# The modulation products of a diffusion layer take silu(c) from PSUM, and the projections share six banks

## The chip, the cores and the metric

The kernel runs on one core of a Trainium2 chip. The metric is device time in microseconds (us); the times below are of whole executions, and the profile is of one further execution. The engines are called as in the profile: PE (TensorE) with its weight loads PEld, DVE (VectorE), ACT (ScalarE), POOL (GpSimd) and SP (SyncE), whose queue issues most of the DMAs. PSUM has eight banks; a bank holds 512 float32 values for each of 128 partitions.

## The reference

One layer works on 1024 latent tokens and 256 context tokens, with 1024 channels, in float32. What matters here is the first part:

```python
mod = jax.nn.silu(c) @ w_mod[l] + b_mod[l]
shift1, scale1, gate1, shift2, scale2, gate2 = jnp.split(mod[:, None, :], N_MOD, axis=-1)
...
mod_c = jax.nn.silu(c_ctx) @ w_mod[l, :, :n_mod_c * D_MODEL] + b_mod[l, :n_mod_c * D_MODEL]
...
h_c = ctx * (1.0 + mods_c[1]) + mods_c[0]
kv_ctx = _context_kv(h_c, w_in[l], b_in[l], k_norm_g[l])
h = x * (1.0 + scale1) + shift1
y = _latent_token_mixer(h, kv_ctx, w_in[l], b_in[l], attn_sink[l], q_norm_g[l], k_norm_g[l],
                        w_branch_a[l], w_branch_b[l], w_out[l], rope)
```

So a vector of 1024 values, silu(c), is multiplied with a matrix of 1024 x 6144 (and silu(c_ctx) with its first 2048 columns). The results scale and shift the tokens. The mixer then projects the tokens to queries, keys, values and gate logits (`proj = h @ w_in + b_in`), runs two attentions (a windowed one, A, and a global one, B), and merges them by sigmoid gates. An output projection, a layer norm, a convolutional feed-forward part and a second layer norm follow; the change does not touch these.

## The kernel before

**Precision.** Every large product is made of three matmuls on rounded parts (`mm3`, L379 to L381): high x high, high x low and low x high. `split` (L371, L376) makes the parts: a cast gives the high part, a subtraction the low one.

**The products with silu(c)** do not go through PE. `mod` (L478, L479) is one DVE instruction: it multiplies a tile of 128 x 1024 modulation weights, in SBUF, with silu(c) spread over all partitions (`sc`, or `scc` for the context's vector, both 128 x 1024 in SBUF), adds the bias and sums each partition's row into one column of `modc` or `modx`. There are 64 such columns. The first 16 (scale1 and shift1) are made in `modulate` (L501) at the very start, since the projections need them. The other 48 (`late`, first 16 with `scc`, then 32 with `sc`) are spread over the projections: `mods` (L941) is called after each step of PE work and issues as many products as are due, so that all are traced by the end of group ka. `mload` (L935) loads the next weight tile on SP when a product has been issued.

**The start.** PE spreads c over the partitions with a matmul against ones into two tiles `cb`, ACT makes silu of each half into `sc`, and warm-up matmuls run into `cb[1]` and into a tile `warm`.

**The projections**, in PE's order: first q of branch B ("q1acc", eight tiles of 128 tokens, weights stepped over eight channel blocks k); then gates ("g", each gate block in two halves of 512 tokens, 24 matmuls a half), and between them qa and qb (q of branch A, four tiles each), ka (keys and values of tokens 0 to 639, five tiles) and kb (tokens 640 to 1023 and the context, five tiles). `GORD` (L39) sets it: 3 gate blocks, qa, 4, qb, 4, ka, 1, kb, 3 (a fourth is kept for attention). So the halves are 6, 8, 8, 2 and 6. A group's tiles are all open from its first step to its last.

**Evictions.** A gate half is evicted by ACT's sigmoid (L967). q tiles are evicted by DVE at the end of their group (L607, L609). A key tile runs through `kv_post` (L670): s1 evicts it (DVE, L675) and makes sums of squares and the rotation of half of it; s2 finishes norm and rotation and splits the keys (L375, L376); s3 turns them by four PE transposes into a tile `ktr` (L706) that ACT copies away (L709, L711). `side_step` (L979) advances these pieces by one step after each PE step, and after ka the transposes of the first two units' queries (`qtr`, L741) go through the same queue. In the program the side steps stand so that ktr0 comes ahead of kb, ktr1 after kb's first step, ktr2 and qtr0 after its second, ktr3 and qtr1 after its third, ktr4 after its fourth.

**PSUM.** All these tiles come from `acc_tile` (L439): pool `ps1` has one tag with eight slots of one bank, and the framework gives a tile any slot that is free. When ps1 is released (L1064), attention's pool ps2 takes the banks.

**What sets the order.** The framework orders each engine's instructions at compile time, by the program's order and by when it reckons an instruction can start. Where a block of `manual_schedule` stands, the program's order is kept: for DVE and SP from the end of q1 to the end of ka (L1006, L1018), and for all engines in attention, which a planner in the kernel orders. PE's and ACT's orders in the projections, and DVE's after ka, are the framework's. Weights are loaded five steps ahead of their use (WLOAD) and split three steps ahead (WSPLIT).

## Time and profile before

| | |
|---|---|
| median of 3 runs | 1515.82 us (1514.42 to 1516.7) |
| span of the profiled execution | 1514.0 us |
| PE busy | 1501.8 us, 7584 matmuls |
| DVE busy | 1154.9 us |
| ACT busy | 799.4 us |
| POOL busy | 782.8 us |
| the 48 late products on DVE | 60.6 us to 243.4 us |

The profile is one execution. Busy time is the time in which an engine had an instruction of the program under way; a matmul's end is modelled, and matmuls overlap, so the distance between two starts tells more of PE's pace than the duration. A row of a group reads: line, engine, operation, tiles written and read (numbers left out), shapes, count, then busy us and mean ns of one, then the engine's idle time just before and what ended it. A row of a tile's view gives the shortest, median and longest duration in ns, and the first and last start in us. A timeline row gives start and duration in us. A row of a window gives its length and each engine's busy us with its number of instructions.

### The profile page before, as it was taken

Reading aid. Unit: us, or ns where it says so; the run is one execution under the profiler, and the core shown is the slowest. Engines: PE = TensorE matmul, PEld = TensorE weight load, DVE = VectorE, ACT = ScalarE, POOL = GpSimd, SP = SyncE. Lnnn points to the kernel's source line nnn. Section 1 sums busy time; section 2 is a strip of 40 time slices with the busy share of each in tenths; the row PEclk is TensorE's granted clock in tenths of the full one; section 3 lists DMA queues with packets and bytes.
Section 4 is the critical chain, followed back from the end, with each engine's and each line's share of the span. In section 5 each row is a group of like instructions: output and inputs, shape, how many; then the busy total and the mean of one; then the engine's idle time right before and its main releaser. Section 6 shows DMA issues by size and latency. Waiting matters only on the chain.

```text
span 1514.0 us, 21879 instructions
## 1 busy us (share of the span) xinstructions
PE 1501.8 (99%) x7584; PEld 1261.5 (83%) x7584; DVE 1154.9 (76%) x1735; ACT 799.4 (53%) x1406; POOL 782.8 (52%) x744
## 2 busy tenths in 40 slices
PE   9999999999999999999999999999999999999997
PEld 7888888889888888888888998888888888888886
DVE  7588847629887777787666888988888888657897
ACT  6422223449987777788233665444444444435533
POOL 0374303439996666576424446666676774021063
PEclk9999999999999999999999999999999999999999
DMA  9767773312447555623460322333344447996723
GB/s 377 269 211 257 223 238 108 99 42 68 125 135 180 147 119 139 148 60 117 141 166 22 113 89 98 112 111 112 112 111 112 112 111 199 367 271 205 252 83 112
DMA packets 112432, 229.84 MB, mean 152 GB/s; under 512 B 13537, under 2 KB 27617, under 8 KB 112226
## 3 DMA queue, kind: packets, MB, share of 16 engines
q1 hardware_dynamic: 97312, 199.85, 40.5%
q0 software_dynamic: 10400, 20.19, 8.6%
q10 hardware_dynamic: 4610, 8.42, 1.5%
q8 instruction: 59, 0.97, 0.3%
q14 instruction: 51, 0.42, 0.1%
HBM read 177.23 MB, written 65.87 MB: 161 GB/s over the span
## 4 chain that ended last, share of the span: by engine, by line
PE 94%; DVE 3%; issue 1%; DMA 1%; ACT 1%; POOL 0%; DVEq 0%; SPq 0%; ACTq 0%; POOLq 0%
PE av L864 7%; PE pt L855 7%; PE g L379 4%; PE g L380 4%; PE g L381 4%; PE s L762 3%; PE p L380 3%; PE s L763 3%; PE p L381 3%; PE p L379 3%; PE c L381 2%; PE d L381 2%; PE a L381 2%; PE d L379 2%; PE a L379 2%; PE c L380 2%
## 5 line engine op out<-in xcount | busy, mean ns | idle before, releaser
L1253 DVE TENSOR_TENSOR lo<-pt,hi 128x512 fp32r<-128x512 f32 x188 | 127.0, 687 | 47.7 <-ACT hi L1247 36.8
L376 DVE TENSOR_TENSOR ld<-rd,hd 128x1024 fp32r<-128x1024 f32 x77 | 97.6, 1285 | 49.6 <-ACT hd L371 47.5
L1247 ACT CAST hi<-pt 128x512 fp32r<-128x512 f32 x188 | 108.2, 583 | 41.1 <-PE av L864 23.6
L371 ACT CAST hd<-rd 128x1024 fp32r<-128x1024 f32 x77 | 79.5, 1050 | 86.3 <-PE p L381 57.6
L380 PE MATMUL p<-ld,hd 128*128 128x512 f32 x264 | 102.9, 390 | 0.6 <-DVE ld L376 0.6
L379 PE MATMUL p<-hd 128*128 128x512 f32 x264 | 103.3, 391 | 0.0
L381 PE MATMUL p<-hd,ld 128*128 128x512 f32 x264 | 102.8, 390 | 0.0
L864 PE MATMUL av<-hi,VT 128*128 128x512 f32 x236 | 101.1, 431 | 0.2 <-POOL hi L1242 0.2
L379 PE MATMUL g<-hh,whg 128*128 128x512 f32 x256 | 99.9, 390 | 0.0
L864 PE MATMUL av<-lo,VT 128*128 128x512 f32 x236 | 99.5, 428 | 0.2 <-POOL lo L1253 0.2
L380 PE MATMUL g<-hl,whg 128*128 128x512 f32 x256 | 99.7, 390 | 0.0
L381 PE MATMUL g<-hh,wlg 128*128 128x512 f32 x256 | 99.7, 389 | 0.0
L376 POOL TENSOR_TENSOR wlg<-wg,whg 128x512 fp32r<-128x512 f32 x32 | 45.4, 1423 | 100.8 <-ACT whg L371 88.4
L801 DVE TENSOR_SCALAR_CACHE_REDUCE p<-s,cvt,nmc 128x1024 f32<-128x1024 f32 x64 | 85.6, 1339 | 7.3 <-PE pt L855 4.3
L810 ACT ACTIVATE p<-p,nm 128x1024 f32<-128x1024 f32 x64 | 74.0, 1156 | 8.0 <-DVE p L801 7.9
L855 PEld LDWEIGHTS pt<-ident,p 128*128 128x128 f32 x512 | 63.5, 140 | 17.6 <-ACT rb L837 0.4
L855 PE MATMUL pt<-ident,p 128*128 128x128 f32 x512 | 76.6, 272 | 0.1
L762 PE MATMUL s<-KL,q 128*128 128x512 f32 (+2 forms) x186 | 73.8, 397 | 0.0
L371 ACT CAST wS<-s 128x512 fp32r<-128x512 f32 x76 | 45.2, 620 | 50.8 <-POOL s L1583 50.0
L763 PE MATMUL s<-KL,q 128*128 128x512 f32 (+2 forms) x186 | 69.6, 374 | 0.0
L371 ACT CAST wA<-ru 128x512 fp32r<-128x512 f32 x57 | 35.5, 623 | 62.3 <-PE d L381 34.1
L1253 POOL TENSOR_TENSOR lo<-ptr,hi 128x512 fp32r<-128x512 f32 x48 | 62.2, 1296 | 3.3
(437 smaller groups left out, 5007.0 us busy)
## 6 DMA issues: line engine op xcount, KB each, us to landing
wml<-in_wmodT_dram SPq DMA_DIRECT2D x48, 512.0 KB
ru<-in_w_up_dram SPq DMA_DIRECT2D x38, 512.0 KB
rd<-td SPq DMA_DIRECT2D x55, 256.0 KB
rd<-sd SPq DMA_DIRECT2D x44, 256.0 KB
rd<-in_w_dn_dram SPq DMA_DIRECT2D x33, 256.0 KB
wm<-in_wmodT_dram SPq DMA_DIRECT2D x16, 512.0 KB
wg<-in_w_g_dram SPq DMA_DIRECT2D x32, 256.0 KB
q<-q SPq DMA_DIRECT2D x64, 128.0 KB
```

Source lines behind the costliest of these rows:

```text
L371: cast[:] = [nc.scalar.copy(hi, src).ins]
L376: low[:] = [lo_eng.tensor_tensor(out=lo, in0=src, in1=hi.bitcast(F32), op=ALU.subtract).ins]
L379: nc.tensor.matmul(ps, a[0], b[0], start=start, stop=False, skip_group_check=resumed)
L380: nc.tensor.matmul(ps, a[0], b[1], start=False, stop=False, skip_group_check=resumed)
L381: return nc.tensor.matmul(ps, a[1], b[0], start=False, stop=stop, skip_group_check=resumed).ins
L762: nc.tensor.matmul(o, self.q1[:, hs], ks, start=True, stop=False)
L763: nc.tensor.matmul(o, self.q2[:, hs], ks, start=False, stop=stop)
L801: nc.vector.tensor_scalar(out=p if self.br else p[:, self.pad + 1:SINK + 1], in0=self.sv[h], scalar1=self.scale()[:, hs] if self.br else - ...
L855: nc.tensor.transpose(tr[:, h * P:(h + 1) * P], src, ident)
L864: nc.tensor.matmul(self.av, v, self.parts[n][low], start=first, stop=self.left == 0)
L1247: nc.scalar.copy(hi, units[u].parts[n])
L1253: e.tensor_tensor(out=lo, in0=src, in1=hi.bitcast(F32), op=ALU.subtract)
```

## The change

The PSUM pool gets named tags: six of one bank, used in turn by `acc_tile`, and one, "wide", of two banks. The wide tile serves first the two halves of `cb`, then the last two of q1's eight tiles, and then, in the late products, silu(c_ctx) and after it silu(c): ACT copies the row from SBUF into it, in two halves, when the first product with that row is issued (products 0 and 16 of the 48), and the products read it there. The 16 products at the start still read `sc` in SBUF.

```diff
-    ps1 = tc.alloc_tile_pool(name="ps1", bufs=8, space=PSUM, reuse_waits="tile")
+    ps1 = tc.alloc_tile_pool(name="ps1", bufs=1, space=PSUM, reuse_waits="tile")
+    abanks = list(range(6))
 
     def acc_tile(name, dt=F32):
-        return ps1.tile([P, 512], dt, tag="acc", name=name)
+        n = abanks.pop(0)
+        abanks.append(n)
+        return ps1.tile([P, 512], dt, tag=f"acc{n}", name=name)
+
+    def wide_tile(name):
+        return ps1.tile([P, T], F32, tag="wide", name=name)
...
-    cb = [acc_tile(f"cb{n}") for n in (0, 1)]
+    cbw = wide_tile("cb")
+    cb = [cbw[:, n * HALF:(n + 1) * HALF] for n in (0, 1)]
...
-    acc = [acc_tile(f"q1acc{t}") for t in range(NT)]
+    acc = [acc_tile(f"q1acc{t}") for t in range(6)]
+    accw = wide_tile("q1accw")
+    acc += [accw[:, n * HALF:(n + 1) * HALF] for n in (0, 1)]
...
+    crows = {}
+
+    def crow_psum(row, nm):
+        t = wide_tile(nm)
+        for n in (0, 1):
+            nc.scalar.copy(t[:, n * HALF:(n + 1) * HALF], row[:, n * HALF:(n + 1) * HALF])
+        return t
+
     def mods(us):
...
             col, row, o, w = coming.pop(0)
-            mod(w, row, bmc[:, col:col + 1], o)
+            if (col, row) in ((0, scc), (16, sc)):
+                crows[0] = crow_psum(row, f"cp{col}")
+            mod(w, crows[0], bmc[:, col:col + 1], o)
```

## The prediction

> **What bounds the kernel now.** I read the page's busy times and the chain that ended last, then the busy time by stage, then the single tiles of the projections.

> ```profile
> span 1514.0 us, 21879 instructions
> PE   1501.8 (99%) x7584; PEld 1261.5 (83%) x7584; DVE 1154.9 (76%) x1735; ACT 799.4 (53%) x1406; POOL 782.8 (52%) x744
> ```

> ```profile
> core 0: us, PE busy (x) PEld busy (x) DVE busy (x) ACT busy (x) POOL busy (x), PEclk, DMA share, GB/s
> 0.00:54.00 54.00, 52.92 (x219) 42.42 (x220) 38.43 (x67) 30.82 (x35) 4.34 (x17) 1.00 0.86 323
> 54.00:255.00 201.00, 201.00 (x889) 166.43 (x888) 142.69 (x250) 53.42 (x87) 82.20 (x67) 1.00 0.67 225
> 255.00:333.00 78.00, 78.00 (x385) 65.13 (x384) 38.98 (x122) 31.00 (x86) 28.15 (x39) 1.00 0.24 76
> 333.00:1460.00 1127.00, 1125.85 (x5833) 948.94 (x5832) 891.84 (x1232) 666.29 (x1170) 641.59 (x601) 1.00 0.50 139
> 1460.00:1514.00 54.00, 44.06 (x266) 38.53 (x264) 43.00 (x67) 17.90 (x30) 26.50 (x22) 0.95 0.23 78
> ```

> A PE share of 99% need not mean that PE is the limit, so the pace has to be seen too. In 54 to 255 us, where all 48 products lie, 889 matmuls stand in 201.0 us: 0.226 us each. Neighbours in the timeline start 0.23 us apart, so nothing makes one wait:

> ```profile
> 58.19 0.39 PE L379 MATMUL g<-hh,whg 128*128 128x512 f32 x1
> 58.42 0.39 PE L380 MATMUL g<-hl,whg 128*128 128x512 f32 x1
> ```

> The stages that the change touches end at 333 us, where ps1 has been given back and attention runs in its written order. Up to there PE is idle for 54.00 - 52.92 = 1.08 us, all in the first window, and for nothing after 54 us. A helper that gets faster here can win 1.08 us at most. A helper or a bank that comes late costs its whole delay.

> **The change part by part.** *The 48 products.* Their rows, by group and by single durations:

> ```profile
> L479 DVE CUSTOM_DVE_ANT_0 wml<-wml,sc,bmc 128x1024 f32<-128x1024 f32 x32 | 47.6, 1517 | 0.0
> L479 DVE CUSTOM_DVE_ANT_0 wml<-wml,scc,bmc 128x1024 f32<-128x1024 f32 x16 | 21.2, 1346 | 5.3 <-DMA wml<-in_wmodT_dram 5.3
> L479 DVE CUSTOM_DVE_ANT_0 wml<-wml,sc,bmc x32: 1274/1280/2342, 120.6 to 242.1; 128x1024 f32<-128x1024 f32 x32
> L479 DVE CUSTOM_DVE_ANT_0 wml<-wml,scc,bmc x16: 1271/1280/2315, 60.6 to 119.4; 128x1024 f32<-128x1024 f32 x16
> ```

> Half of them take 1.28 us, some 2.3 us. The cause of the long ones is not in a row by itself. If a product that reads one operand from PSUM is never held up, the saving is 32 x (1.517 - 1.280) + 16 x (1.346 - 1.280) = 7.6 + 1.1 = 8.7 us of DVE time. Whether the operand in PSUM is slower by itself I take from two subtractions of one size, the first with an operand in PSUM, the second with both in SBUF:

> ```profile
> L1253 DVE TENSOR_TENSOR lo<-pt,hi 128x512 fp32r<-128x512 f32 x45 | 30.1, 683 | 4.5 <-ACT hi L1247 4.2
> L376 DVE TENSOR_TENSOR wlka<-wka,whka 128x512 fp32r<-128x512 f32 x8 | 5.5, 691 | 23.1 <-ACT whka L371 23.1
> L376 POOL TENSOR_TENSOR wlg<-wg,whg 128x512 fp32r<-128x512 f32 x32 | 45.4, 1423 | 100.8 <-ACT whg L371 88.4 <-DMA wg<-in_w_g_dram 11.8 <-PE q1acc L381 0.6
> ```

> 683 and 691 ns: no difference, so I take 1.28 us for each new product. [...] On the path to the end the saving counts 0 either way: PE covers it, and there is no PE gap in the window to close. POOL waits 88.4 us for ACT's casts ahead of its subtractions, so it is not late either.

> *The copies.* Two rows of silu(c), two halves each, are four ACT copies. The nearest row:

> ```profile
> L1237 ACT COPY ptr<-pt 128x512 f32<-128x512 f32 x12 | 7.1, 590 | 3.3 <-PE pt L855 3.0 <-POOL qs L736 0.2
> L609 DVE TENSOR_TENSOR Q<-q1acc,bias_qb x8: 680/680/691, 51.4 to 55.6; 128x512 f32<-128x512 f32 x8
> 120.64 1.28 DVE L479 CUSTOM_DVE_ANT_0 wml<-wml,sc,bmc 128x1024 f32<-128x1024 f32 x1
> 138.89 1.16 DVE L376 TENSOR_TENSOR wlqb<-wqb,whqb 128x512 fp32r<-128x512 f32 x1 [4.61 <-ACT whqb L371]
> ```

> 4 x 0.59 = 2.4 us of ACT, which is busy 53.42 of 201. The first pair can start when q1's last two tiles are evicted (55.6 + 0.7 = 56.3 us) and is done near 57.5; the first product started at 60.6. The second pair waits for the sixteenth product, and the seventeenth (120.64) for the copies: DVE, whose order is written by hand here, stands for 1.2 us and two handovers, say 1.5 us, with the next products, the rotations of q and the weight splits queued behind. What hides that is DVE's wait of 4.61 us for the cast at 138.89; if ACT does the copies one gate late (24 x 0.226 = 5.4 us), DVE is some 1 us late for a weight that PE reads three steps later. Product slots come free as much later, and SP's loads behind them, by the same 1.5 us, less what the products save. I count 0.

> *Six banks, up to 244 us.* The ring's tiles in order are one warm-up tile, six of q1, six gate halves, four of qa, eight gate halves, four of qb, eight gate halves, five of ka. The tightest reuse is the third gate half after qa, which takes the bank of qa's first tile:

> ```profile
> L381 PE MATMUL accqa<-whqa,hl x32: 388/389/390, 87.0 to 108.1; 128*128 128x512 f32 x32
> L607 DVE SCALAR_TENSOR_TENSOR Q<-accqa,bias_qa x4: 676/676/679, 113.3 to 115.1; 128x512 f32<-128x512 f32 x4
> ```

> It starts two gate halves behind the end of qa, 108.1 + 0.2 + 2 x 5.4 = 119.1 us; that tile is evicted at 113.3 + 0.7 = 114.0. A margin of 5 us: 0.

> *Six banks, 255 to 310 us.* Following the ring on gives for kb5 to kb9 the banks of ka2, ka3, ka4 and of the two gate halves, and then for ktr2, qtr0, ktr3, qtr1 and ktr4 the banks of kb5 to kb9. In the order of the program, kb7 asks for a bank before ka4's eviction is traced, and the five transposes ask for banks that are held to the end of kb.

> ```profile
> 255.46 0.46 PE L379 MATMUL acckb<-whkb,hh 128*128 128x512 f32 x1
> 256.90 0.39 PE L379 MATMUL acckb<-whkb,hh 128*128 128x512 f32 x1
> L675 DVE TENSOR_TENSOR kv<-accka,bias_kv x5: 678/684/691, 243.5 to 259.9; 128x512 f32<-128x512 f32 x5
> L675 DVE TENSOR_TENSOR kv<-acckb,bias_kv x5: 676/692/692, 282.5 to 297.3; 128x512 f32<-128x512 f32 x5
> L706 PE MATMUL ktr<-identr,ks x40: 221/247/253, 255.2 to 308.5; 128*128 128x128 f32 x40
> ```

> Kept in program order, kb7's first matmul (the seventh of kb, 256.90) would wait for ka4's eviction at 259.9 + 0.7 = 260.6: 3.7 us. Nothing of its own order is written by hand for PE here, though; kb8, kb9 and the second step of four tiles are 6 + 12 matmuls, 4.1 us of other work. The end that excludes a loss is then 0. That PE's order does move late matmuls back shows at the start, where by the program each L381 follows its L379 and L380 at once:

> ```profile
> L379 PE MATMUL q1acc<-whqb,hh x64: 387/389/640, 10.1 to 53.2; 128*128 128x512 f32 x64
> L381 PE MATMUL q1acc<-whqb,hl x64: 388/389/396, 11.9 to 53.7; 128*128 128x512 f32 x64
> ```

> The first L381 comes 1.8 us behind the first L379, and PE loses at most 1.08 us in that whole window. For the transposes: they go behind the evictions of kb, which the before has from 282.5 to 298.0. The keys are wanted when attention begins, and before that come the gate halves after kb, six times 5.4 us. The gate half that needs ktr3's bank is the third (from 255.5 + 120 x 0.226 + 2 for transposes = 284.6, so 284.6 + 10.8 = 295.4), and kb7's eviction, the third of five, lies near 290. What is left is that the order is fixed at compile time and DVE may run later than it was planned, since some steps ahead of those evictions are stretched:

> ```profile
> L572 DVE TENSOR_TENSOR ktp<-kv,tbk x8: 275/282/825, 249.6 to 294.1; 128x128 f32<-128x128 f32 x8
> L599 DVE TENSOR_TENSOR kv<-kv,ssk x10: 277/292/1373, 249.0 to 301.6; 128x128 f32<-128x128 f32 x10
> L375 DVE CAST ks<-kv x10: 280/286/1359, 250.6 to 302.4; 128x256 fp32r<-128x256 f32 x10
> L376 DVE TENSOR_TENSOR ks<-kv,ks x10: 410/416/1391, 250.9 to 303.8; 128x256 fp32r<-128x256 f32 x10
> ```

> One stretched step of each kind is 0.54 + 1.08 + 1.07 + 0.98 = 3.7 us, the upper end for the transposes. Between 0 and 3.7 for kb7 and 0 and 3.7 for them I take 0.5 each, near the low end: the row nearest in kind is the first window, which loses 1.08 us at the very most under an order of the same making, but with POOL busy 4.34 of 54 us against 28.15 of 78 here.

> *The ends.* At the start, if the two banks of the wide tile were waited for as one, the second half's product would wait for the first SiLU, 0.6 us. At the hand-over to attention, if the first scores get the bank of the last gate half, they wait for its sigmoid, 319.74 + 0.69 - 319.54 = 0.9 us. The banks of each are separate, and two of four score tiles can lie on the wide tile, free when the last product is done (242.1 + 1.3): 0 for both, with 0.6 and 0.9 as upper ends.

> ```profile
> 3.51 3.78 PE L528 MATMUL cb<-crow,onesf 1*128 1x512 f32 x4
> 5.62 0.60 ACT L529 ACTIVATE sc<-cb 128x512 f32<-128x512 f32 x1 [2.65 <-PE cb L528]
> 319.54 0.28 PE L762 MATMUL s<-KL,q 128*128 128x256 f32 x1
> 319.74 0.69 ACT L967 ACTIVATE sg<-g,bgc 128x512 f32<-128x512 f32 x1 [4.76 <-PE g L381]
> ```

> *Sum.* 0 + 0 + 0 + 0.5 + 0.5 + 0 = +1.0 us: the span goes from 1514.0 to 1515.0. The median of the runs, 1515.82, lies 1.8 us above the profiled span; I add 1.0 to it: 1516.8. The bounds are -1.1 (all idle ahead of 54 us gone) and 3.7 + 3.7 + 0.6 + 0.9 = +8.9.

> **The rivals.** *Slower: banks bound by name.* Before, any free one of eight banks served the next tile; now a tile waits for one certain bank while others stand empty. Place: kb7 and the five transposes, 255 to 300 us. Price: up to 3.7 + 3.7 = 7.4 us (1523.2), half of it 3.7 (1519.5). It decides from 3.0 us of stops on, which is 0.2% of the time and about what a measurement here can tell from no change. For it: PE has no slack to catch up, and the stretched DVE steps. Against it: the other matmuls at hand. Chance 0.28.

> *Faster: the products give the path time back.* If DVE or POOL set PE's pace in 54 to 255 us, the 8.7 us would come off: 1507.1. [...] Against the rival stands the window with PE busy 201.00 of 201.00. Chance 0.05.

> *It doesn't do what it says:* the products stay as long as they were, since something else stretches them. DVE then gains nothing and ACT still copies; the time is the same 1516.8. Chance 0.10.

> **How the numbers follow.** The forecast as worked out has 0.57. Same is 0.57 + 0.10 = 0.67, slower 0.28, faster 0.05. The range goes down to 1514.2 (1515.82 less 1.1, and less half a microsecond of spread between runs) and up to 1521.0, which takes in the bank rival to some two thirds of its price.

> **What would show it.** Products near 1.28 us without the long ones, DVE's busy time 6 to 9 us down, four new ACT copies of 0.6 us; PE's window 54 to 255 still full; no ktr group between ktr1 and the first eviction of kb. PE idle in 255 to 333 above 3 us makes the forecast wrong on one side; a matmul pace below 0.226 us, or attention that begins before 319 us, on the other.

## The result

The changed kernel takes 1530.32 us (median of 4 runs, 1529.99 to 1530.34); the kernel before, run beside it, 1515.15 (4 runs, 1514.42 to 1516.7). The ratio is 1.0096, 95% interval 1.0085 to 1.0108: 15.2 us slower. The forecast was 1516.8, with a range up to 1521.0.

The span and the engines' busy time of the changed kernel, from its page:

```profile
span 1528.5 us, 21888 instructions
PE   1508.3 (99%) x7584; PEld 1263.8 (83%) x7584; DVE 1138.3 (74%) x1735; ACT 801.5 (52%) x1410; POOL 774.6 (51%) x744
```

DVE is 16.6 us less busy and POOL 8.2 us, and the program is 14.5 us longer. Same windows as before (length, busy us of each engine, granted clock, DMA share, GB/s):

```profile
0.00:54.00 54.00, 50.14 (x199) 39.52 (x200) 35.51 (x62) 28.85 (x33) 4.28 (x17) 1.00 0.86 322
54.00:255.00 201.00, 201.00 (x889) 166.46 (x888) 129.63 (x230) 54.89 (x88) 70.34 (x66) 1.00 0.66 224
255.00:333.00 78.00, 72.13 (x327) 57.77 (x326) 40.19 (x137) 27.98 (x78) 27.28 (x35) 0.96 0.26 76
```

The window with the products is as full as it was, 201.00 of 201.00. The loss lies on both sides of it: PE is idle for 3.86 us in the first window and for 5.87 us in the third, where it was idle for 1.08 and 0, and the granted clock of the third is 0.96. The added idle time (3.86 + 5.87 - 1.08) is 8.7 us of the 14.5, so there must be slower work as well. The milestones, side by side (starts in us, from the timelines):

| | before | after | longer by |
|---|---|---|---|
| first q1 matmul | 10.07 | 13.23 | 3.2 |
| first gate matmul | 53.89 | 58.38 | 1.3 more |
| first kb matmul | 255.46 | 259.96 | 0 more |
| first attention score | 319.54 | 334.64 | 10.6 more |
| end | 1513.95 | 1528.55 | 0.5 back |

**The start.** PE's timeline in the changed kernel: start and duration in us, count, and in brackets the idle time before and what ended it:

```profile
3.38 1.06 PE L539 MATMUL warm<-onesf 128*128 128x128 f32 x4
4.37 2.07 PE L535 MATMUL cb<-crow,onesf 1*128 1x512 f32 x2
6.37 2.08 PE L539 MATMUL warm<-onesf 128*128 128x128 f32 x8
8.37 2.07 PE L535 MATMUL cb<-crow,onesf 1*128 1x512 f32 x2
13.23 0.80 PE L379 MATMUL q1acc<-whqb,hh 128*128 128x512 f32 x1 [2.79 <-ACT hh L523]
13.82 0.63 PE L380 MATMUL q1acc<-wlqb,hh 128*128 128x512 f32 x1
14.25 0.63 PE L379 MATMUL q1acc<-whqb,hh 128*128 128x512 f32 x1
```

The two SiLU in ACT's timeline of the same kernel:

```profile
6.47 0.60 ACT L536 ACTIVATE sc<-cb 128x512 f32<-128x512 f32 x1 [3.51 <-PE cb L535]
10.48 0.60 ACT L536 ACTIVATE sc<-cb 128x512 f32<-128x512 f32 x1 [2.90 <-PE cb L535]
```

Two things have changed. (The profile holds two records for each of these float32 matmuls: 12 for the six that write warm.) Two of the six warm-up matmuls stand ahead of the first half of cb, and the second half no longer follows the first at once (3.51 to 7.29 for both, before): it starts at 8.37, after the SiLU of the first half (6.47 + 0.60) and after the other four warm-up matmuls, behind which the compiled order put it. The second SiLU is 3.2 us late (10.48 against 7.32), and so are the first tokens and q1. PE stands for 2.79 us, and then q1's matmuls start 0.43 us apart instead of 0.23 until 16.4: half pace, 1.3 us more by the first gate matmul. Whether that is the clock, this profile's column of the granted clock doesn't say. It reads 1.00 over the slow matmuls of the changed kernel (first row), but 0.50 over matmuls of the same pace in named_eight, a kernel described below (second row):

```profile
13.30:16.30 3.00, 3.00 (x7) 2.44 (x8) 2.72 (x7) 3.00 (x6) 0.00 (x0) 1.00 1.03 396
9.80:13.80 4.00, 4.00 (x9) 2.84 (x10) 3.36 (x7) 3.14 (x6) 0.00 (x0) 0.50 0.96 371
```

The end of the slow pace also differs a little between kernels that begin alike: four of those below have the changed kernel's order up to q1, and their first gate matmul starts at 58.6 to 58.9 us, where the changed kernel's starts at 58.38.

**255 to 335 us.** PE of the changed kernel at its stops:

```profile
261.20 0.50 PE L379 MATMUL acckb<-whkb,hh 128*128 128x512 f32 x1 [0.32 <-DVE kv L684]
...
263.95 0.37 PE L715 MATMUL ktr<-identr,ks 128*128 128x128 f32 x2
265.92 0.79 PE L379 MATMUL acckb<-whkb,hh 128*128 128x512 f32 x1 [1.61 <-DVE kv L684]
266.51 0.63 PE L380 MATMUL acckb<-wlkb,hh 128*128 128x512 f32 x1
266.94 0.63 PE L381 MATMUL acckb<-whkb,hl 128*128 128x512 f32 x1
...
295.57 0.39 PE L381 MATMUL g<-hh,wlg 128*128 128x512 f32 x1
299.26 0.53 PE L715 MATMUL ktr<-identr,ks 128*128 128x128 f32 x4 [3.30 <-DVE kv L684]
299.63 0.64 PE L379 MATMUL g<-hh,whg 128*128 128x512 f32 x1
300.07 0.63 PE L380 MATMUL g<-hl,whg 128*128 128x512 f32 x1
...
306.45 0.54 PE L715 MATMUL ktr<-identr,ks 128*128 128x128 f32 x4 [0.53 <-DVE kv L684]
```

Of the two longest, the first is kb7's first product, the second ktr3. Both are released by an eviction of a key tile (L684). The gate matmuls that stand behind ktr3 need nothing of it, but they stand behind it in the compiled order, and none of them starts before 299.63. Which evictions these two are, DVE's timeline shows:

```profile
265.18 0.68 DVE L684 TENSOR_TENSOR kv<-accka,bias_kv 128x512 f32<-128x512 f32 x1
...
298.00 0.41 DVE L376 TENSOR_TENSOR ks<-kv,ks 128x256 fp32r<-128x256 f32 x1
298.33 0.21 DVE L587 TENSOR_TENSOR ktp<-kv,tbk 128x64 f32<-128x64 f32 x1
298.51 0.69 DVE L684 TENSOR_TENSOR kv<-acckb,bias_kv 128x512 f32<-128x512 f32 x1
```

The last of ka (ka4) and the third of kb (kb7): the tiles whose banks kb7 and ktr3 are bound to in the ring. The second stands right behind the split (L376) of an earlier tile's keys; that returns below. With shorter stops of 0.32, 0.09 and 0.53 us, PE stands for 5.85 us in this stage. The other 4.8 of the 10.6 us are slower work. Part of it is the granted clock (the first number after POOL's count), in windows laid behind the two stops:

```profile
266.00:269.00 3.00, 3.00 (x9) 2.31 (x10) 3.00 (x13) 2.12 (x8) 1.51 (x2) 0.50 0.19 55
299.70:303.10 3.40, 3.40 (x11) 2.63 (x10) 2.81 (x11) 1.06 (x6) 1.55 (x2) 0.51 0.00 1
```

13 matmuls of kb and the gates start 0.43 us apart there instead of 0.227: 2.6 us. The rest, some 2 us, lies at the first instruction behind each stop and at the transposes. Not all of that is the clock: six_free, below, loses 1.4 us beyond the length of its stops, with the clock at 1.00.

The products did what was said of them (shortest, median and longest in ns, from the tile's view):

```profile
L485 DVE CUSTOM_DVE_ANT_0 wml<-wml,cp,bmc x48: 1266/1276/1281, 63.8 to 246.6; 128x1024 f32<-128x1024 f32 x48
```

### The profile page after: what moved, and what is told of

Same layout as the page of the kernel before. It is cut to its first block, busy times and chain, and to the rows that moved or that the text cites. A ratio compares the mean times of both kernels' runs of the same rounds, so it can differ in the third digit from the quotient of the medians.

```text
span 1528.5 us, 21888 instructions
## 1 busy us (share of the span) xinstructions
PE 1508.3 (99%) x7584; PEld 1263.8 (83%) x7584; DVE 1138.3 (74%) x1735; ACT 801.5 (52%) x1410; POOL 774.6 (51%) x744
## 4 chain that ended last, share of the span: by engine, by line
PE 91%; DVE 5%; DMA 1%; issue 1%; POOL 1%; ACT 1%; SPq 0%; DVEq 0%; ACTq 0%; POOLq 0%
PE av L873 7%; PE pt L864 7%; PE g L379 3%; PE g L381 3%; PE g L380 3%; PE s L771 3%; PE s L772 3%; PE p L379 2%; PE p L381 2%; PE p L380 2%; PE c L380 2%; PE d L380 2%; PE a L380 2%; PE c L379 2%; PE a L379 2%; PE d L379 2%
## 5 line engine op out<-in xcount | busy, mean ns | idle before, releaser
L376 DVE TENSOR_TENSOR ld<-rd,hd 128x1024 fp32r<-128x1024 f32 x77 | 96.6, 1272 | 51.2 <-ACT hd L371 49.0
L371 ACT CAST hd<-rd 128x1024 fp32r<-128x1024 f32 x77 | 79.4, 1049 | 87.3 <-PE p L381 56.4
L376 POOL TENSOR_TENSOR wlg<-wg,whg 128x512 fp32r<-128x512 f32 x32 | 41.9, 1316 | 121.7 <-ACT whg L371 107.1
L379 PE MATMUL p<-hd 128*128 128x512 f32 x264 | 103.3, 391 | 0.0
L380 PE MATMUL p<-ld,hd 128*128 128x512 f32 x264 | 103.1, 390 | 0.3 <-DVE ld L376 0.3
L381 PE MATMUL p<-hd,ld 128*128 128x512 f32 x264 | 102.8, 389 | 0.0
L379 PE MATMUL g<-hh,whg 128*128 128x512 f32 x256 | 100.8, 394 | 0.0
L380 PE MATMUL g<-hl,whg 128*128 128x512 f32 x256 | 100.4, 392 | 0.0
L381 PE MATMUL g<-hh,wlg 128*128 128x512 f32 x256 | 100.3, 392 | 0.0
L371 ACT CAST wS<-s 128x512 fp32r<-128x512 f32 x76 | 45.2, 620 | 50.8 <-POOL s L1602 49.9
L371 ACT CAST wA<-ru 128x512 fp32r<-128x512 f32 x57 | 35.5, 623 | 62.5 <-PE d L381 34.1
L485 DVE CUSTOM_DVE_ANT_0 wml<-wml,cp,bmc 128x1024 f32<-128x1024 f32 x48 | 60.0, 1275 | 8.7 <-DMA wml<-in_wmodT_dram 7.6
```

The costliest lines, as they stand in the source:

```text
L371: cast[:] = [nc.scalar.copy(hi, src).ins]
L376: low[:] = [lo_eng.tensor_tensor(out=lo, in0=src, in1=hi.bitcast(F32), op=ALU.subtract).ins]
L379: nc.tensor.matmul(ps, a[0], b[0], start=start, stop=False, skip_group_check=resumed)
L380: nc.tensor.matmul(ps, a[0], b[1], start=False, stop=False, skip_group_check=resumed)
L381: return nc.tensor.matmul(ps, a[1], b[0], start=False, stop=stop, skip_group_check=resumed).ins
```

## The experiments

The theory after the comparison: the loss comes from banks that are bound by name and in turn, and from the two halves of cb in one tile; the products have no part in it. Rivals: six banks are too few; the copies and products disturb ACT's or DVE's order; the half clock is the main loss and needs only the stops to be filled. Differences below are of the medians, each to the kernel before as it ran beside that experiment; the changed kernel stands at +15.2 us.

**cb_two_tiles**: the halves of cb in two tiles.

```diff
-    cbw = wide_tile("cb")
-    cb = [cbw[:, n * HALF:(n + 1) * HALF] for n in (0, 1)]
+    cb = [acc_tile(f"cb{n}") for n in (0, 1)]
```

> The changed kernel, with the two halves of the spread c in two one-bank tiles again; the rest of the change stays. Theory (the second half's matmul waits for ACT's SiLU of the first half, because both halves are one tile): the first projection matmul comes near 10.1 us instead of 13.2 and the first gate near 53.9 instead of 58.4, so 4.5 us come off: about 1525.8. Rival (the start is late for another reason, such as the order of the first projection's last two tiles): the first gate stays near 58.4 and the time near 1530.3.

1528.95 us, ratio 1.0088 (1.0071 to 1.0105): +13.3. PE at the start:

```profile
3.37 1.06 PE L538 MATMUL warm<-onesf 128*128 128x128 f32 x4
4.36 3.78 PE L534 MATMUL cb<-crow,onesf 1*128 1x512 f32 x4
8.07 2.08 PE L538 MATMUL warm<-onesf 128*128 128x128 f32 x8
10.92 0.79 PE L379 MATMUL q1acc<-whqb,hh 128*128 128x512 f32 x1 [0.78 <-ACT hh L523]
```

The halves follow each other again, and q1 begins 2.3 us earlier than in the changed kernel: it was the shared tile that held the second half back. About half of it is lost again, as the slow pace lasts longer (first gate matmul at 57.18, 1.2 us earlier). The time moved by less than the two intervals can tell apart. Two warm-up matmuls are still ahead of cb, so the shared tile isn't needed for that.

**six_free**: the names taken away, six slots of one tag, as the eight were before; cb still in the wide tile.

```diff
-        n = abanks.pop(0)
-        abanks.append(n)
-        return ps1.tile([P, 512], dt, tag=f"acc{n}", name=name)
+        return ps1.tile([P, 512], dt, tag="acc", name=name, bufs=6)
```

> The changed kernel, with one tag of six slots in place of six named banks: a tile takes any of the six that is free; the wide tile, the copies and the products stay. Theory (what costs 10.6 us between 255 and 335 is that tiles are bound to certain banks): the transposes of keys and queries stand between the steps of kb again, PE has no wait over 1 us there, and the time falls by 9 to 11 us to about 1520. Rival (six banks are too few, whoever picks them): the waits stay, and the time stays within 3 us of 1530.

1523.01 us, ratio 1.0052 (1.0037 to 1.0067): +7.4, half of the loss gone. PE's stops from 255 to 335 us:

```profile
263.34 0.50 PE L379 MATMUL acckb<-whkb,ch 128*128 128x512 f32 x1 [0.62 <-ACT sg L984]
266.32 0.53 PE L713 MATMUL ktr<-identr,ks 128*128 128x128 f32 x4 [1.01 <-DVE kv L682]
272.14 0.53 PE L748 MATMUL qtr<-identr,qs 128*128 128x128 f32 x4 [0.48 <-ACT KL L716]
276.72 0.50 PE L748 MATMUL qtr<-identr,qs 128*128 128x128 f32 x4 [0.16 <-ACT KL L716]
```

2.27 us of stops instead of 5.85, none long, and the granted clock stays at 1.00. The theory's 9 to 11 us did not come off in full: the time is 7.8 us below the changed kernel's. From kb's first matmul to attention it takes 67.7 us (64.1 before, 74.7 changed). What is left there, 3.6 us, is put down to six slots in place of eight; turns_in_wide tests that.

**cb_and_free**: both edits.

> Both edits together: two one-bank tiles at the start and six slots that are chosen freely; silu(c) still comes from the two-bank tile for all 48 products. Theory (start and named banks are the whole loss, and the products' 9 us on DVE are covered by PE): the two gains add up, 4.5 + 10.6 = 15.1, and the time is that of the kernel before, 1515.2, within 2 us. Rival (the products or copies cost or gain by themselves): 1517 or more, or under 1513.

1520.5 us, ratio 1.003 (1.0018 to 1.0042): +4.9. q1 begins at 10.08 as before, with all warm-up matmuls behind cb. So named tags and the shared tile each put two of them first: cb_two_tiles has them there with names alone, and six_free with the shared tile alone:

```profile
3.37 1.06 PE L537 MATMUL warm<-onesf 128*128 128x128 f32 x4
```

q1's pace is half up to 12.4, and the first gate matmul starts 0.9 us later than before, though the order up to q1 is the same. The stage from kb to attention is 67.8 us, 3.7 us longer than before, much as in six_free. The expected 1515.2 was missed by these two parts. The rival of this run, that products or copies cost something, is what turns_in_wide and turns_sbuf decide.

**silu_sbuf**: the changed kernel with its products reading SBUF, without the copies.

```diff
-                crows[0] = crow_psum(row, f"cp{col}")
+                crows[0] = row
```

> The changed kernel, but the 48 products read silu(c) in SBUF as before, and the four copies are left out; the named banks and the wide tile for the spread c and the last two tiles of the first projection stay. Theory (the products lie beside PE work and the loss is all in the tiles): 1530.3 within 2 us, with DVE busy 7 to 9 us more than in the changed kernel. Rival (the copies, or the earlier products, shift the order and make the loss): the time falls by 5 us or more toward 1515.

1528.85 us, ratio 1.009 (1.0075 to 1.0105): +13.2, not told apart from the changed kernel. The stops are the same (2.79 us at the start, then 2.02 before kb7, where the changed kernel has 0.32 + 0.09 + 1.61, and 3.30 before a ktr), although the long products are back (up to 2.35 us). The products and copies are not the loss.

**named_eight**: the kernel before with eight named banks in turn, and nothing else of the change.

```diff
-    ps1 = tc.alloc_tile_pool(name="ps1", bufs=8, space=PSUM, reuse_waits="tile")
+    ps1 = tc.alloc_tile_pool(name="ps1", bufs=1, space=PSUM, reuse_waits="tile")
+    abanks = list(range(8))
...
-        return ps1.tile([P, 512], dt, tag="acc", name=name)
+        n = abanks.pop(0)
+        abanks.append(n)
+        return ps1.tile([P, 512], dt, tag=f"acc{n}", name=name)
```

> The kernel before with one edit: its eight slots get names and are used in turn; no wide tile, no copies, products from SBUF. Theory (names are the loss, not the count of six): following the ring, kb9 takes ka4's bank, ktr3, qtr1 and ktr4 take those of kb5 to kb7, and the first two gate halves after kb take those of kb8 and kb9, so PE stops behind kb's evictions by 8 us or more and the time is 1521 to 1528. Rival (six banks are too few, names do no harm where there are eight): 1515 within 2 us.

1526.33 us, ratio 1.0069 (1.0054 to 1.0084): +10.7. Its stops in the same stage:

```profile
262.41 0.50 PE L379 MATMUL acckb<-whkb,ch 128*128 128x512 f32 x1 [2.04 <-DVE kv L679]
295.39 0.53 PE L710 MATMUL ktr<-identr,ks 128*128 128x128 f32 x4 [2.88 <-DVE ks L376]
299.69 0.50 PE L379 MATMUL g<-hh,whg 128*128 128x512 f32 x1 [0.56 <-DVE kv L679]
```

Eight banks are enough when any free one serves, and cost 10.7 us when each tile has its own: the names do it with no bank taken away. Some 8.0 us of it lie between kb and attention and 1.9 ahead of the first gate matmul, where this kernel has a stop of 2.48 us before q1. Behind the stop of 2.04 us the clock is half:

```profile
263.40:266.60 3.20, 3.20 (x11) 2.55 (x10) 2.81 (x11) 1.06 (x5) 1.43 (x2) 0.50 0.23 55
```

The stop of 2.88 us is of another kind. It ends with the split of the very keys that are turned, an operand, and not with an eviction:

```profile
294.92 0.41 DVE L376 TENSOR_TENSOR ks<-kv,ks 128x256 fp32r<-128x256 f32 x1
```

These are the transposes of kb's first tile (ktr5). They stand 8 gate matmuls behind kb's last matmul here, and 48 behind it in the kernel before, where they wait for nothing. So names cost in two ways: a tile waits for one certain bank, and PE's compiled order comes out differently.

**turns_one_bank**: the changed kernel with all ktr and qtr from ktr1 on in ktr0's bank, and the other five banks in turn for the rest.

```diff
-        n = abanks.pop(0)
-        abanks.append(n)
+        if name.startswith(("ktr", "qtr")):
+            n = abanks[0] if name == "ktr0" else tbank[0]
+            tbank[:] = [n]
+            if n in abanks:
+                abanks.remove(n)
+        else:
+            n = abanks.pop(0)
+            abanks.append(n)
```

> The changed kernel with named banks, but from ktr0 on the transposes of keys and queries all use one bank, and the other five go round for kb and the gates. Theory (the stop of 3.3 us and the half clock after it come from transposes that were given kb's banks): that stop goes, what stays is kb7's wait for ka4's eviction, and the time falls by 5 to 8 us to 1522 to 1525. Rival (the stop belongs to late evictions as such, whatever the transposes take): within 3 us of 1530.

1524.08 us, ratio 1.0051 (1.0036 to 1.0066): +8.5. The stop of 3.30 us is gone with its half clock, as the transposes no longer wait for kb. The stop of 1.61 us before kb7 stays, with 3.4 us of half clock behind it (0.50 from 266.2 to 269.2 us).

**kv_three**: the changed kernel with three buffers in SBUF for the evicted keys and values, not two (and one for the sigmoid's tile, not two, to make room).

```diff
-KVB = 2
+KVB = 3
...
-            sg = ph1.tile([P, HALF], F32, tag="sg", name=f"sg{f}_{hf}", bufs=2)
+            sg = ph1.tile([P, HALF], F32, tag="sg", name=f"sg{f}_{hf}", bufs=1)
```

> After with three buffers for k and v instead of two, and one for the sigmoid's tile to make room for them. Theory: the eviction of kb7's product, which ends the 3.30 us stop before a k transpose, came late because its kv buffer was still being read by an earlier chunk. Then that stop and the 3.41 us at half clock behind it go, the stop of 1.61 us before kb7 may stay: about 4 to 6 us less than after, 1524 to 1526. Rival: the eviction was late only because VectorE had other work queued ahead of it, or the bank was bound: within 2 us of 1530.

1524.59 us, ratio 1.0056 (1.004 to 1.0073): +9.2. The third eviction of kb in DVE's timeline:

```profile
292.18 0.68 DVE L684 TENSOR_TENSOR kv<-acckb,bias_kv 128x512 f32<-128x512 f32 x1
```

PE's stops in the same stage:

```profile
262.69 0.50 PE L379 MATMUL acckb<-whkb,hh 128*128 128x512 f32 x1 [0.73 <-DVE kv L684]
292.91 0.53 PE L715 MATMUL ktr<-identr,ks 128*128 128x128 f32 x4 [1.49 <-DVE kv L684]
297.60 0.50 PE L750 MATMUL qtr<-identr,qs 128*128 128x128 f32 x4 [1.56 <-DVE kv L684]
```

The eviction stands at 292.18 instead of 298.51: with two buffers it had to wait for the second step (norm, rotation, split) of an earlier tile to give one back. ka4's eviction too comes earlier (262.0 instead of 265.2), and the stop before kb7 is halved. So behind a named bank stood a chain: PE waits for a bank, the bank for its eviction, and the eviction for a buffer in SBUF. The same two buffers cost PE nothing before, where the transposes up to ktr4 are done ahead of kb's first eviction (271.0 against 282.5 us). The stops that are left end with evictions too: later evictions still hold banks. The sigmoid's single buffer is a second edit; no stop of PE in this stage ends with a sigmoid.

**warm_fill**: the changed kernel with six more warm-up matmuls that read silu(c), so that they lie in the stop ahead of q1.

```diff
+    for n in range(6):
+        nc.tensor.matmul(wt_[:, 0:P], onesf, sc[:, 0:P], start=True, stop=True)
```

> The changed kernel with six more warm-up matmuls that read the first half of silu(c) and so run behind the second half's matmul, in the 2.8 us in which PE stands idle. Theory (the first projection matmuls run at half speed because the clock is not yet granted after that idle time): they start at the same 13.2 us, but 0.23 us apart instead of 0.43, and 1 to 2 us come off: about 1529. Rival (the 0.43 us is a wait for operands, not the clock): no change within 0.5 us.

1526.45 us, ratio 1.0072 (1.0056 to 1.0089): +10.8, a larger gain than either theory gave it. PE's timeline at the start tells why it can't be put down to the edit alone:

```profile
4.37 1.27 PE L535 MATMUL cb<-crow,onesf 1*128 1x512 f32 x2
5.57 1.16 PE L539 MATMUL warm<-onesf 128*128 128x128 f32 x8
6.66 1.12 PE L535 MATMUL cb<-crow,onesf 1*128 1x512 f32 x2
7.71 2.58 PE L541 MATMUL warm<-sc,onesf 128*128 128x128 f32 x12
```

Up to this point the order is that of the changed kernel, but the two matmuls at 4.37 take 1.27 us instead of 2.07: full pace came before the added matmuls began. q1 starts at 10.57 us, not at 13.2, and behind its first two matmuls it runs 0.23 us apart. Later its stop of 1.62 us before kb7 was followed by no half clock, while the one of 3.30 us was. What the filling is worth by itself stays open.

**turns_in_wide**: six free slots, cb in two tiles, the wide tile in a pool of its own that is released after the last product; its two banks then serve ktr and qtr.

```diff
+        if len(psw) > 1 and name.startswith(("ktr", "qtr")):
+            return psw[1].tile([P, 512], dt, tag="turn", name=name)
+        return ps1.tile([P, 512], dt, tag="acc", name=name, bufs=6)
...
-        return ps1.tile([P, T], F32, tag="wide", name=name)
+        return psw[0].tile([P, T], F32, tag="wide", name=name)
...
+                psw[0].release()
+                psw.append(tc.alloc_tile_pool(name="psx", bufs=2, space=PSUM, reuse_waits="tile"))
```

> Six freely chosen slots, two one-bank tiles at the start, all 48 products from the two-bank tile as in the run with both edits; once the last product is done the wide tile is given back and its two banks serve the transposes of keys and queries, so that kb has eight banks again. Theory (what that run still lost, 3.7 us between kb and attention, is the two banks that are missing): kb to attention takes 64 us again and the time is 1515 to 1517. Rival (the rest is the order that the framework chose): 1519 or more.

1516.91 us (10 runs), ratio 1.0008 (0.9998 to 1.0017): +1.3. One stop of 0.60 us is left in the stage, which takes 65.5 us, 1.4 more than before. The products are still short, and the kernel is not faster than before.

**turns_sbuf**: the same, with the products reading SBUF.

> turns_in_wide (six free slots, the two halves of cb in two tiles, the wide tile given back after the last product and its banks used for the transposes) with the products reading silu(c) from SBUF as in the kernel before, without the PSUM copies. Theory: the 9 us that the products take less on VectorE and GpSimd with one operand in PSUM are worth nothing, since TensorE has no idle time there: 1516.9 within 1.5 us. Rival: the products do matter at the end of the stage: 2 us or more slower than turns_in_wide. Second rival: ScalarE's copies cost something on the path: 1.5 us or more faster.

1516.36 us (11 runs), ratio 1.0007 (0.9999 to 1.0016): +0.95. The products of this kernel in the tile's view:

```profile
L487 DVE CUSTOM_DVE_ANT_0 wml<-wml,sc,bmc x32: 1272/1280/2346, 121.7 to 243.2; 128x1024 f32<-128x1024 f32 x32
L487 DVE CUSTOM_DVE_ANT_0 wml<-wml,scc,bmc x16: 1269/1279/2307, 61.5 to 120.5; 128x1024 f32<-128x1024 f32 x16
```

And those of turns_in_wide:

```profile
L487 DVE CUSTOM_DVE_ANT_0 wml<-wml,cp,bmc x48: 1266/1276/1281, 61.4 to 242.9; 128x1024 f32<-128x1024 f32 x48
```

DVE is 11.3 us less busy with the copies in PSUM (1139.9 against 1151.2), and the differences to the kernel before lie 0.35 us apart, inside both intervals. What the change was to win is worth nothing on the path here. No version was found that beats the kernel before.

Put in a row, each difference to the kernel before:

| kernel | us |
|---|---|
| changed | +15.2 |
| names taken away (six_free) | +7.4 |
| and cb in two tiles (cb_and_free) | +4.9 |
| and transposes in the wide tile's banks (turns_in_wide) | +1.3, not told apart from 0 |

The intervals of the second and third row just overlap (1.0037 to 1.0067 and 1.0018 to 1.0042), so the size of that step is loose; those of the other steps do not overlap.

## Why the prediction was wrong

*Right.* The products: 1.276 us each, none long. With 60.0 us busy for the group against 68.8, they save 8.8 us where 8.7 was worked out. All nine long products of the kernel before (1.75 to 2.34 us) overlap a GpSimd (POOL) instruction with two inputs in time. So do 13 of the 39 short ones (1.27 to 1.32 us), and the GpSimd instruction beside such a one can be long: the split at 234.81 us took 1.95 us, and the one at the same place in the changed kernel, at 239.31, took 1.30. In the changed kernel 21 of the 48 products overlap a GpSimd instruction, and none is long (1.281 us at most). The long ones go with the operand's place (2.353 us at most in silu_sbuf and 2.346 in turns_sbuf, 1.281 in the changed kernel and turns_in_wide); by what mechanism, no run shows. DVE's whole busy time fell by 16.6 us, not by 6 to 9. The part beyond the products isn't theirs: silu_sbuf, whose products read SBUF as before, is 7.9 us below the kernel before as well (1147.0 against 1154.9). The 6 us at the lower end allowed for a product that is slower with an operand in PSUM; no run shows that (1.276 us in the changed kernel, against a median of 1.280 before). That the saving is worth 0 on the path is shown twice, by silu_sbuf and by turns_sbuf. The copies took 0.59 us each and cost DVE one wait of 1.1 us, and nothing on PE. Six banks up to 244 us: 0, as forecast. The hand-over to attention: 0 (0.5 us less from the first score to the end).

*The failed step* is "Six banks, 255 to 310 us", where kb7 and the transposes were given 0.5 us each, "near the low end". The places were right, and so was the rival that named them (chance 0.28). Standing time came out at 2.02 us for kb7 and its neighbours (0.32 + 0.09 + 1.61) and at 3.83 us for the transposes (3.30 + 0.53), beside bounds of 3.7 for each. The reason for the low end was the first window of the kernel before, where PE's compiled order moved late matmuls back. That order was made with eight free slots. Under names, kb7 and ktr3 stood in PE's order ahead of the evictions they need, with matmuls behind them that need neither. For kb7 the prediction counted 18 matmuls of other work; PE's order has the 6 of kb8 and kb9 ahead of it, and the second step behind it, while ka4's eviction ended 5.9 us after kb's first matmul instead of 5.1. For ktr3 it gave room up to the third gate half behind kb, that is 48 matmuls; ktr3 stands behind 12. PE idle above 3 us in the third window was named as the mark of a wrong forecast; it is 5.87. The upper bound for the transposes, one stretched step of DVE, was also not the right price: kv_three shows a wait for an SBUF buffer in it.

*The missing terms.* A stop was priced at its own length. In this stage 5.85 us of stops cost 10.6. The clock fell to half behind two of them, for 3.4 us each, which can cost 3.4 us together at most (an estimate: half of 6.8); and a stop costs more than its length even at the full clock (1.4 us over the four of six_free). No term allowed for either. With the 4.8 us that they cost here, the bank rival's 7.4 would have been 12.2.

*The start* was put at 0 with an upper end of 0.6 us, and cost 4.5. The mechanism had been named: the second half of cb is held behind the first SiLU if the wide tile counts as one, and cb_two_tiles shows that it does. But the price was that of the wait alone (0.6), and not of what comes ahead of it in PE's order: four warm-up matmuls (6.37 to 8.4) between the halves, two more ahead of the first, and a stop of 2.79 us and q1 at half pace behind them. cb_two_tiles moves q1 forward by 2.3 us by itself, and cb_and_free brings it back to where it was. Some of the 4.5 us is pace that the order doesn't decide: cb_and_free, with the order of the kernel before up to q1, is 0.9 us behind it at the first gate matmul.

That names lead the compiled order to these places is shown (named_eight, and six_free without them). How the framework reckons there, and why it put ktr3 ahead of gate matmuls that could have run, stays open.

## What to carry to other kernels

Giving each tile a certain buffer turns "any free one" into a wait for one eviction, and on an engine that runs in compiled order everything behind that wait stands too (none of the gate matmuls behind ktr3 started before 299.63): look for the last of each named buffer's readers, and for what those readers wait for in turn. Two uses that only share a tile are ordered by it: here the write of the second half (from 8.37 us) waited for the read of the first (6.47 + 0.60). And on a path that one engine fills to 201.00 of 201.00 us, time saved on a helper can be worth nothing, as the 8.8 us on DVE were here, while buffers taken from that engine are paid for: the two missing banks cost some 3.6 us (4.9 in cb_and_free less 1.3 in turns_in_wide).

## What the runs showed of the hardware

```profile
295.40:299.00 3.60, 3.60 (x20) 2.79 (x20) 3.01 (x13) 1.95 (x10) 1.63 (x2) 1.00 0.19 65
```

What decides besides the length was not shown: no run moves a stop and leaves the rest as it is. Why the same two matmuls at 4.37 us take 2.07 us in the changed kernel and 1.27 in warm_fill was not shown either. Stops of 1.6 us were followed by half clock in three profiles of four.
